# Four attention query tiles fewer, rotary halves exchanged on the keys, FFN operands normalised in place, and a finer start

## The chip, the cores and the metric

The kernel runs on one core of a Trainium2 chip. TensorE (PE) multiplies matrices into PSUM banks; VectorE (DVE), ScalarE (ACT) and GpSimd (POOL) work on tiles in SBUF; SyncE (SP) and POOL issue transfers. PEld is PE's loading of weights, which runs beside its matmuls. The metric is device time in microseconds (us) from start to end of one execution. Each engine runs its own instructions in the order in which the program's scheduler has written them, and waits for others through semaphores.

## The reference

One inference step of two layers on 384 tokens of 1024 features: 128 context tokens and 256 latent ones. Layer 0 has multi-head latent attention, layer 1 a Mamba-2 scan; each layer has a feed-forward network (FFN) of half weight before and after its mixer. Cut to what matters here:

```python
def ffn_half(x, shift, scale, gate, g, w_in, w_out):
    return x + 0.5 * gate * swiglu(adaln_input(x, g, shift, scale), w_in, w_out)
def adaln_input(x, g, shift, scale):
    return rmsnorm(x, g) * (1 + scale) + shift
def mla_project(h, w_in, q_norm, kv_norm, wq_b):
    q_a, kv_a, k_r = jnp.split(h @ w_in, [Q_LORA, Q_LORA + KV_LORA], axis=-1)
    q = (rmsnorm(q_a, q_norm) @ wq_b).reshape(b, l, MLA_HEADS, QK_HEAD)
# latent tokens: the last 32 of a head's 96 query columns, and the one rotary key, are turned
def apply_axial_rope(x, cos, sin):
    rot = jnp.stack([-xr[..., 1, :], xr[..., 0, :]], axis=-2)
    return (xr * cos + rot * sin).reshape(x.shape).astype(x.dtype)
# attention: softmax(q k / sqrt(96)) v, 16 heads; latent tokens see context and latent keys
```

All weights and data are float32. shift, scale and gate come from SiLU(cond) times a matrix of 18 sections of 1024 columns, for two conditions (context and latent).

## The kernel before

Features lie on the partitions, tokens in the columns. Stages follow each other: FFN 0.0, attention (`mla`), FFN 0.1, FFN 1.0, the scan layer (`ssm`), FFN 1.1. Every weight tile of 128 x 128 is streamed from memory in units of eight (`raw`, SP's queue), split into a rounded part and a rest (`whi` by ACT, `wlo` by DVE: `stream_split`, three units ahead), and the moving operand is split too (`xh` and `xl`), so that one product takes three matmuls, lines 124 to 126 in `wmm`: xh by wlo, xl by whi, xh by whi.

An FFN has 44 input tiles of 8 x 3 matmuls (`in_tile`) and 8 output tiles of 22 x 3 (`fo`). xh and xl hold x times (1 + scale) times g, made tile by tile when the residual of the stage before is added (`prep_x`), plus two columns with the shift, one for each kind of token: 386 columns. The RMS factor comes later (`norm_stat`: three small matmuls `rs`, a few column operations, and `spread`, a matmul `rb` that spreads them over the partitions, copied to `rext`); `evac` multiplies each result by `rext` and adds the shift's columns. `in_first_pair` runs the first two tiles so that `rs` can stand behind seven k steps. Between tiles DVE makes sums for later sections of the modulation (`mod_steps`, line 183; `Fill` spreads them). mla has the eight columns 56 to 64 of these.

At the start the first two sections are made on PE in four rounds (`mod_round`, 2 MB of `mod01` each), and three pairs of input tiles (`head`) run two k steps behind each round.

In mla, `q_a` makes the low-rank query operand without its RMS factor; a second `rstd` spreads it, and `rq` holds it times the rotary table. A query tile holds one head: 64 plain rows, 32 rotary ones, and the same 32 with halves exchanged, so one product with `rq` (`q_scale`) turns and normalises; the key tile `kext` repeats the turned key. The loop runs over eight pairs of heads: `kq` (key tile `k`, 6 matmuls; from pair 2 on two query tiles `q` of 12), then for each head transposes of the pair before (`ta`, `tb`), `scores` (`s0`, `s1`), softmax on DVE and ACT (`mx`, `p`, `sm`), and `pv`.

Of the kernel before, what the change touches and what calls it, by code (L numbers as in the profile page):

```python
# [15 lines left out]
P = 128  # L16
# [5 lines left out]
NX = 386  # L22
DFF = 2816
# [10 lines left out]
N_UNITS = 4 * FFN_UNITS + 27 + 57  # L34
MOD_SECS = 18

# [10 lines left out]
for _name, _n in (("ident", 128), ("ones", 128), ("triu", 128), ("tril", 128), ("sup", 128), ("slo", 128), ("sel", 4)):  # L47
    _TAB[_name] = (_off, _off + _n)
    _off += _n
# [4 lines left out]
def kernel(ctx, tc, xT_d, wstream, mod01, modw, crow_d, cst_d, tab_d, rope_d, ckvT_d, krT_d, h0_d,  # L54
# [13 lines left out]

    cst = pers.tile([P, N_CST], F32, tag="cst", name="cst")
    tab = pers.tile([P, N_TAB], F32, tag="tab", name="tab")  # L70
    xT = pers.tile([P, KT, NTOK], F32, tag="xT", name="xT")
    xh = pers.tile([P, KT, NX], F32R, tag="xh", name="xh")
    xl = pers.tile([P, KT, NX], F32R, tag="xl", name="xl")
    mod = pers.tile([P, 144, 2], F32, tag="mod", name="mod")
    gs = pers.tile([P, KT, 2], F32, tag="gs", name="gs")
    hg = pers.tile([P, KT, 2], F32, tag="hg", name="hg")
    cst32 = pers.tile([P, KT, 32], F32, tag="cst32", name="cst32")
    acc = pers.tile([P, NTOK], F32, tag="acc", name="acc")
    rext = pers.tile([P, NX], F32, tag="rext", name="rext")
    dg = pers.tile([P, NTOK], F32, tag="dg", name="dg")  # L80
# [10 lines left out]
    nc.vector.memset(cst32, 0.0)  # L91
# [39 lines left out]
    def mod_round(r, pool):  # L131
        raw = pool.tile([P, KT, 512], F32, tag="mod01", name=f"mod01_{r}", bufs=4)
        for i in range(4):
            nc.sync.dma_start(raw[:, 2 * i:2 * i + 2, :], mod01[r][:, 2 * i:2 * i + 2, :])

        def run():
            ks = slice(2 * r, 2 * r + 2)
            ps = bank(f"psmod_{r}")
            for kt in range(KT):
                g = kt % 4  # L140
                mm(ps[32 * g:32 * g + 32, :], cst32[:, kt, :], raw[:, kt, :], start=(kt < 4), stop=(kt >= 4),  # L141
                   tile_position=(0, 32 * g))
            sb = pool.tile([P, 512], F32, tag="modsb", name=f"modsb_{r}", bufs=2)
            nc.scalar.copy(sb, ps)
            yield
            pt = bank("modT")
            for q in range(4):
                nc.tensor.transpose(pt[:, q * P:(q + 1) * P], sb[:, q * P:(q + 1) * P], T("ident"))
            red = pool.tile([P, 4, 2], F32, tag="modred", name=f"modred_{r}", bufs=2)
            nc.vector.tensor_reduce(out=red, in_=pt.rearrange("p (b g z) -> p b z g", b=4, g=4)[:, :, 0:2, :],  # L150
                                    axis=AX.X, op=ALU.add)
            dst = mod[:, 0:2 * KT, :].rearrange("p (c k) s -> p c k s", c=2)
            mb = C("modb", 0, 2 * KT).rearrange("p (c k) -> p c k", c=2)
            for i in range(2):
                tt(out=dst[:, :, ks, i], in0=red[:, :, i].rearrange("p (c k) -> p c k", c=2), in1=mb[:, :, ks], op=ALU.add)
            prep_scale(0, 0, ks)
            prep_shift(0, 0, ks)
            for kt in (2 * r, 2 * r + 1):
                prep_x(kt)
            yield  # L160
        return run()
# [51 lines left out]
    def rstd(sq, inv_n, out):  # L213
# [3 lines left out]
        v, r, w = (pers.tile([P, 3], F32, tag=f"rs{i}", name=f"rs{i}", bufs=2) for i in range(3))  # L217
# [5 lines left out]
        stt(out=r, in0=w, scalar=1.5, op0=ALU.add, in1=r, op1=ALU.mult)  # L223
        for c in range(3):
            ts(out=dg[:, c * P:(c + 1) * P], in0=T("ident"), scalar1=r[:, c:c + 1], scalar2=None, op0=ALU.mult)
# [49 lines left out]
    def in_tile(keyf, m):  # L275
        ps = bank("in")
        for k in range(KT):
            wmm(ps[:, :NX], keyf(m, k), xh[:, k, :], xl[:, k, :], k == 0, k == KT - 1)
# [19 lines left out]
    def head_mm(keyf, tiles, k0):  # L298
        for m, ps in tiles:
            for k in (k0, k0 + 1):  # L300
# [836 lines left out]
```

## Time and profile before

| | |
|---|---|
| median of 3 runs | 1695.97 us (1695.53 to 1696.38) |
| the profiled execution | 1695.77 us, its span 1694.0 us |
| busy share of the span | PE 98%, DVE 74%, ACT 47%, POOL 12% |
| mean granted clock of PE | 0.991 |

A profile shows each instruction's engine, line, tiles and time. Matmuls overlap, so the sum of their durations says more than the time that passes; starts say how fast they follow each other. In a row of a view, `<-` behind the bracket names what ended an engine's idle time, and `x` the number of instructions that are taken together.

### The profile page before, as it was taken

The numbers are of one execution on the slowest core, as the hardware profiler recorded it, in microseconds if no ns is written. First come the engines' busy times: TensorE is split into PE (matmuls) and PEld (weight loads), VectorE is DVE, ScalarE is ACT, GpSimd is POOL, SyncE is SP. The second block draws the span as 40 slices with busy tenths as digits, with TensorE's granted clock in tenths as the row PEclk, the third lists the DMA queues.
The fourth block names the chain that finished last, engine by engine and source line by source line (L and its number), as shares of the span: only waits on it lengthen the run. The fifth ranks groups of instructions, "written<-read, shape, count | busy, mean of one in ns | idle before, by whom it ended". The sixth has DMA issues, their size and how long they took to land.

```text
span 1694.0 us, 25203 instructions
## 1 busy us (share of the span) xinstructions
PE 1655.4 (98%) x9616; PEld 1584.6 (94%) x9631; DVE 1254.1 (74%) x2069; ACT 791.7 (47%) x1308; POOL 196.1 (12%) x180
## 2 busy tenths in 40 slices
PE   7999999999999999999999999999998999999996
PEld 3899999987899999999999999988897999999996
DVE  3798889579868888986888897888876765444443
ACT  3533333455544333334333333787766644333332
POOL 0111100110001111000111100023222201111000
PEclk9999999999999999999999999999998999999998
DMA  9476667443245666664666574354433333333331
GB/s 349 172 228 210 206 203 235 131 151 101 75 164 183 204 206 202 214 229 157 208 205 205 193 241 164 121 166 134 141 122 119 97 125 123 125 125 125 124 125 50
DMA packets 88441, 281.99 MB, mean 166 GB/s; under 512 B 9836, under 2 KB 19900, under 8 KB 87808
## 3 DMA queue, kind: packets, MB, share of 16 engines
q1 hardware_dynamic: 86560, 274.26, 49.6%
q0 software_dynamic: 1104, 5.28, 0.9%
q8 instruction: 75, 1.23, 0.3%
q10 hardware_dynamic: 656, 0.85, 0.1%
q14 instruction: 46, 0.38, 0.1%
HBM read 276.06 MB, written 4.28 MB: 165 GB/s over the span
## 4 chain that ended last, share of the span: by engine, by line
PE 88%; DVE 5%; ACT 4%; DMA 2%; issue 1%; SPq 0%; POOL 0%; DVEq 0%; ACTq 0%
PE in L124 17%; PE in L126 17%; PE in L125 17%; PE fo L124 7%; PE fo L126 7%; PE fo L125 7%; DVE ca L662 2%; DMA cp<-ecum_d 2%; PE so L124 1%; PE so L125 1%; PE so L126 1%; ACT L769 1%; PE psmod L141 1%; PE wo L124 1%; PE pv L548 1%
## 5 line engine op out<-in xcount | busy, mean ns | idle before, releaser
L124 PE MATMUL in<-xh,wlo 128*128 128x386 f32 x1792 | 613.0, 343 | 3.6 <-ACT xh L246 3.1
L109 ACT CAST whi<-raw 128x1024 fp32r<-128x1024 f32 x348 | 365.3, 1050 | 526.2 <-issue 227.0
L126 PE MATMUL in<-xh,whi 128*128 128x386 f32 x1792 | 610.1, 341 | 0.0
L125 PE MATMUL in<-xl,whi 128*128 128x386 f32 x1792 | 608.3, 339 | 0.2 <-DVE xl L248 0.2
L110 DVE TENSOR_TENSOR wlo<-raw,whi 128x1024 fp32r<-128x1024 f32 x348 | 430.5, 1237 | 129.9 <-ACT whi L109 129.6
L124 PEld LDWEIGHTS in<-xh,wlo 128*128 128x128 f32 x1792 | 339.2, 189 | 10.6 <-issue 4.5
L125 PEld LDWEIGHTS in<-xl,whi 128*128 128x128 f32 x1792 | 339.8, 190 | 4.9 <-issue 2.4
L126 PEld LDWEIGHTS in<-xh,whi 128*128 128x128 f32 x1792 | 337.9, 189 | 3.7 <-issue 3.7
L125 PE MATMUL fo<-al,whi 128*128 128x384 f32 x704 | 236.7, 336 | 0.0
L124 PE MATMUL fo<-ah,wlo 128*128 128x384 f32 x704 | 236.7, 336 | 0.0
L126 PE MATMUL fo<-ah,whi 128*128 128x384 f32 x704 | 236.7, 336 | 0.0
L183 DVE CUSTOM_DVE_ANT_0 work<-modraw,crow,cst 128x1024 f32<-128x1024 f32 x144 | 185.3, 1288 | 20.6 <-POOL al L327 19.3
L327 POOL TENSOR_TENSOR al<-work,ah 128x384 fp32r<-128x384 f32 x88 | 111.2, 1263 | 749.6 <-ACT ah L326 736.2
L124 PEld LDWEIGHTS fo<-ah,wlo 128*128 128x128 f32 x704 | 132.0, 187 | 0.0
L125 PEld LDWEIGHTS fo<-al,whi 128*128 128x128 f32 x704 | 132.0, 187 | 0.0
L126 PEld LDWEIGHTS fo<-ah,whi 128*128 128x128 f32 x704 | 132.0, 187 | 0.0
L183 DVE CUSTOM_DVE_ANT_0 workout<-modraw,crow,cst 128x1024 f32<-128x1024 f32 x96 | 123.1, 1282 | 6.5 <-DMA modraw<-in_modw_dram 5.0
L326 ACT CAST ah<-work 128x384 fp32r<-128x384 f32 x88 | 45.3, 514 | 131.0 <-DVE work L324 131.0
L319 DVE TENSOR_TENSOR work<-in,rext 128x386 f32<-128x386 f32 x88 | 49.1, 558 | 69.7 <-PE in L126 67.8
L320 DVE TENSOR_TENSOR work<-in,rext 128x386 f32<-128x386 f32 x88 | 48.8, 554 | 45.3 <-PE in L126 45.3
L322 ACT ACTIVATE work<-work 128x128 f32<-128x128 f32 (+1 forms) x176 | 70.6, 447 | 4.5 <-DVE work L319 4.1
L324 DVE SCALAR_TENSOR_TENSOR work<-work 128x128 f32<-128x128 f32 (+1 forms) x176 | 68.0, 427 | 5.2
(257 smaller groups left out, 1683.4 us busy)
## 6 DMA issues: line engine op xcount, KB each, us to landing
raw<-in_w_dram SPq DMA_DIRECT2D x348, 512.0 KB, 3.8
modraw<-in_modw_dram SPq DMA_DIRECT2D x128, 512.0 KB, 4.4
mod<-in_mod_dram SPq DMA_DIRECT2D x16, 512.0 KB, 9.9
cp<-ecum_d SPq DMA_DIRECT2D x32, 256.0 KB, 5.0
crow<-silu_d POOLq DMA_DIRECT2D x4, 1024.0 KB, 6.1
h<-in_h_dram SPq DMA_DIRECT2D x16, 128.0 KB, 3.4
out_dram<-sto SPq DMA_DIRECT2D x16, 128.0 KB, 2.3
xT<-in_xT_dram SPq DMA_DIRECT2D x4, 384.0 KB, 9.3
```

The source lines that it names most:

```text
L109: nc.scalar.copy(his[u], raws[u])
L110: tt(out=los[u], in0=raws[u], in1=his[u], op=ALU.subtract)
L124: mm(out, wl, rh, start=start, stop=False)
L125: mm(out, wh, rl, start=False, stop=False)
L126: mm(out, wh, rh, start=False, stop=stop)
L183: nc.vector.tensor_tensor_reduce(out=junk(), in0=raw[n], in1=crow[:, s, :], scale=1.0, scalar=C("modb", j), op0=ALU.mult, op1=ALU.add, acc ...
L319: tt(out=g, in0=pg[:, :NX], in1=rext, op=ALU.mult)
L320: tt(out=u, in0=pu[:, :NX], in1=rext, op=ALU.mult)
L322: act(sg[:, a:b], g[:, a:b], AF.Silu, bias=g[:, NTOK + s:NTOK + s + 1])
L324: stt(out=sg[:, a:b], in0=u[:, a:b], scalar=u[:, NTOK + s:NTOK + s + 1], op0=ALU.add, in1=sg[:, a:b], op1=ALU.mult)
L326: nc.scalar.copy(ah[:, j, :], sg)
L327: nc.gpsimd.tensor_tensor(out=al[:, j, :], in0=sg, in1=ah[:, j, :], op=ALU.subtract)
```

## The change

- Start: `mod_round` becomes `FirstMod`, in rounds of one, one, two, two and two k tiles; the six head tiles run one k step at a time; a few matmuls on zeros (`busy`) and an early activation stand ahead.
- FFN: the first tiles (six in FFN 0.0, else four, `first_four`) run as before, k by k. While they run, `normed_x` overwrites xh and xl with the finished operand, RMS factor and shift included. All later input tiles have 384 columns, and their `evac` is one SiLU from PSUM, one product and the split. The first tiles keep the old one as `evac_raw`.
- Layout: rows of xh, xl and rext are 416 elements long, and small pads move the start of tiles.
- mla: twelve query tiles instead of sixteen: a tile `("n", p)` holds the plain rows of two heads, a tile `("r", g)` the rotary rows of four. `turn` multiplies the rotary tile by cos and by sin; `place` moves the rows of each head into its query operand, rows by DMA on POOL's queue and plain rows by ACT, for the pair behind the current one. The keys hold the halves exchanged. The query's RMS factor goes into the exponential as a scale for each token and into the maximum. The spread of it goes. The mod columns of mla go to FFN 0.0 (16 to 64 in place of 16 to 56).

```diff
+    def first_four(keyf, tiles, layer, sub):
+        ps = [bank(f"in{i}") for i in range(4)]
+        for k in range(KT):
+            for m, p in zip(tiles, ps):
+                wmm(p[:, :NX], keyf(m, k), xh[:, k, :], xl[:, k, :], k == 0, k == KT - 1)
+            if k == 1:
+                spread = norm_stat()
+            if k == 3:
+                spread()
+            if k >= 3:
+                for i in (range(4) if k == 3 else (k,)):
+                    normed_x(layer, sub, i)
+        return ps
+
+    def normed_x(layer, sub, k):
+        sh = sec(layer, 3 * sub)
+        t = pers.tile([P, NTOK], F32, tag="sq", name=f"xn{k}", bufs=2)
+        for s, a, b in SEGS:
+            stt(out=t[:, a:b], in0=xT[:, k, a:b], scalar=gs[:, k, s:s + 1], op0=ALU.mult, in1=rext[:, a:b], op1=ALU.mult)
+        for s, a, b in SEGS:
+            act(xh[:, k, a:b], t[:, a:b], AF.Identity, bias=sh[:, k, s:s + 1])
+        for s, a, b in SEGS:
+            stt(out=xl[:, k, a:b], in0=t[:, a:b], scalar=sh[:, k, s:s + 1], op0=ALU.add,
+                in1=xh[:, k, a:b], op1=ALU.subtract)
...
+            def evac(j, pg, pu):
+                sg = scratch(j)
+                act(sg, pg[:, :NTOK], AF.Silu)
+                tt(out=sg, in0=pu[:, :NTOK], in1=sg, op=ALU.mult)
+                product(j, sg)
...
+            def turn(g, pq):
+                turned[g] = mt([P, 2, NTOK], "qr", 1)
+                for x in range(2):
+                    tt(out=turned[g][:, x, :], in0=pq[:, :NTOK], in1=rope[:, x, :], op=ALU.mult)
+
+            def place(p, pq):
+                for i in range(2):
+                    h = 2 * p + i
+                    qs[h] = mt([P, NTOK], "qt", 4)
+                    a = 32 * (h % 4)
+                    for x in range(2):
+                        nc.gpsimd.dma_start(qs[h][64 + 32 * x:96 + 32 * x, :], turned[h // 4][a:a + 32, x, :])
+                    nc.scalar.copy(qs[h][0:64, :], pq[64 * i:64 * i + 64, :NTOK])
...
-                if qs is None:
-                    qs = []
-                    for h in (0, 1):
-                        pqh = bank("q")
-                        q_mm(pqh, 2 * p + h, range(4))
-                        qs.append(q_scale(pqh))
-                return qs
+                if 1 <= p < HEADS // 2 - 1:
+                    if p % 2 and p > 1:
+                        turn((p + 1) // 2, q_tile(("r", (p + 1) // 2)))
+                    place(p + 1, q_tile(("n", p + 1)))
...
-                    act(pt[:, a:b], s, AF.Exp, bias=mx[:, i:i + 1], scale=ATT_SCALE, accum_out=sm[:, i:i + 1])
+                    act(pt[:, a:b], s, AF.Exp, bias=mx[:, i:i + 1], scale=prq[:, i:i + 1], accum_out=sm[:, i:i + 1])
...
-            fill = Fill(mod_steps(mods[0], mods[1], lp, lambda: work[0][:, 896:]), HEADS // 2 - 1, 1)
```

Three places show how the instructions stand. First DVE at the entry of FFN 0.1, before, from the RMS factors (`dg`) to the first results (`work` from the first pair of tiles):

```order
L225 TENSOR_SCALAR dg<-tab,rs_4588 128x128 x3
L110 TENSOR_TENSOR wlo_4603<-raw_4420,whi_4602 128x1024
L110 TENSOR_TENSOR wlo_4633<-raw_4460,whi_4632 128x1024
L110 TENSOR_TENSOR wlo_4664<-raw_4500,whi_4663 128x1024
L319 TENSOR_TENSOR work_4703<-in_4560,rext 128x386
```

And the same place in the changed kernel, its beginning (`xn` is the scratch of `normed_x`, L305 its first and L309 its last pair of instructions):

```order
L237 TENSOR_SCALAR dg<-tab,rs_4581 128x128 x3
L109 TENSOR_TENSOR wlo_4618<-raw_4441,whi_4617 128x1024
L305 SCALAR_TENSOR_TENSOR xn_4626<-xT,gs,rext 128x128
L305 SCALAR_TENSOR_TENSOR xn_4626<-xT,gs,rext 128x256
L305 SCALAR_TENSOR_TENSOR xn_4633<-xT,gs,rext 128x128
L309 SCALAR_TENSOR_TENSOR xl<-xn_4626,mod,xh 128x128
L305 SCALAR_TENSOR_TENSOR xn_4633<-xT,gs,rext 128x256
L309 SCALAR_TENSOR_TENSOR xl<-xn_4626,mod,xh 128x256
```

Between the factors and the first results there were weight splits alone; now there are 32 instructions of `normed_x` more, of which six stand here; the product of the first result stands among them, ahead of the last xl.

Second, PE in the changed kernel at the same entry, in the two tiles behind the first four (`in_4762` is input tile 2, `in_4799` tile 24, which used to stand whole behind it):

```order
L123 MATMUL in_4762<-xh_62,wlo95_4618 128x384
L123 MATMUL in_4799<-xh_62,wlo96_4686 128x384
L124 MATMUL in_4799<-xl_63,whi96_4685 128x384
L125 MATMUL in_4799<-xh_62,whi96_4685 128x384
L123 MATMUL in_4799<-xh_62,wlo96_4686 128x384
L124 MATMUL in_4799<-xl_63,whi96_4685 128x384
L125 MATMUL in_4799<-xh_62,whi96_4685 128x384
L124 MATMUL in_4762<-xl_63,whi95_4617 128x384
L125 MATMUL in_4762<-xh_62,whi95_4617 128x384
```

The first row is k = 4 of tile 2 by xh; six matmuls of tile 24 stand between it and the two that need xl of k = 4. The two tiles stay interleaved so up to k = 7.

Third, POOL's queue in mla. Before, behind the copies of the turned key:

```order
L468 COPY kext_2794<-krot 64x384
L462 DMA out_dram<-kva 128x2x128
L179 DMA crow<-silu_d 128x2048 x2
```

and in the changed kernel:

```order
L535 COPY kext_2828<-krot 64x384
L502 DMA qt<-qr 32x384 x2
L529 DMA out_dram<-kva 128x2x128
L502 DMA qt<-qr 32x384 x30
L186 DMA crow<-silu_d 128x2048
```

The 32 transfers that move turned rows (`qr`) into the query operands (`qt`) stand there in a row, ahead of the load that the next FFN's mod sums need.

## Rows read from the trace of the kernel before

**Rows 1.** The page: span, and busy us (share) of three engines.

```profile
span 1694.0 us, 25203 instructions
PE 1655.4 (98%) x9616; PEld 1584.6 (94%) x9631; DVE 1254.1 (74%) x2069; ACT 791.7 (47%) x1308; POOL 196.1 (12%) x180
```

**Rows 2.** Windows, FFN 0.1 and 1.0, PE alone: busy (instructions), clock, DMA share, GB/s.

```profile
690.00:770.00 80.00, 80.00 (x460) 1.00 0.65 222
800.00:960.00 160.00, 160.00 (x906) 1.00 0.62 202
```

**Rows 3.** Window of one loop pair: busy (instructions) of PE, PEld, DVE, ACT, POOL.

```profile
422.70:434.70 12.00, 12.00 (x73) 9.71 (x72) 11.14 (x30) 6.44 (x18) 0.00 (x0) 1.00 0.25 88
```

**Rows 4.** Timeline of PE, one loop pair: first query matmul, first transpose behind.

```profile
398.74 0.34 PE L124 MATMUL q<-qph,wlo 128*128 128x384 f32 x1
...
402.93 0.49 PE L534 MATMUL ta<-tab,p 128*128 128x128 f32 x3
```

**Rows 5.** Line 183, mod sums in the loop: ns min/median/max, first and last start.

```profile
L183 DVE CUSTOM_DVE_ANT_0 p<-modraw,crow,cst x16: 1272/1277/1285, 382.7 to 448.9; 128x1024 f32<-128x1024 f32 x16
```

**Rows 6.** Timeline of PE, pair 1: last key matmul and the transposes behind.

```profile
376.36 0.40 PE L126 MATMUL k<-ckvh,whi 128*128 128x512 f32 x1
378.33 0.33 PE L534 MATMUL ta<-tab,p 128*128 128x128 f32 x1 [1.57 <-DVE p L526]
```

**Rows 7.** Timeline of PE where the query factors are spread.

```profile
358.07 0.88 PE L229 MATMUL rb<-dg,tab 128*128 128x384 f32 x2
358.50 0.69 PE L484 MATMUL v<-wlo,ckvh 128*128 128x512 f32 x1
```

**Rows 8.** DMA issues on POOL's queue: count, KB each, median us to landing.

```profile
kext<-in_krT_dram POOLq DMA_DIRECT2D x4, 32.0 KB, 2.6
```

**Rows 9.** Timeline of PE at the start.

```profile
5.55 1.92 PE L141 MATMUL psmod<-mod,cst 128*32 128x512 f32 x4 [5.55 <-DMA mod<-in_mod_dram]
8.10 4.45 PE L141 MATMUL psmod<-mod,cst 128*32 128x512 f32 x12 [0.63 <-DMA mod<-in_mod_dram]
...
16.96 0.66 PE L124 MATMUL in<-xh,wlo 128*128 128x386 f32 x1 [3.08 <-ACT xh L246]
...
21.29 0.69 PE L124 MATMUL in<-xh,wlo 128*128 128x386 f32 x1
...
22.71 1.05 PE L141 MATMUL psmod<-mod,cst 128*32 128x512 f32 x4
23.69 0.44 PE L126 MATMUL in<-xh,whi 128*128 128x386 f32 x1
```

**Rows 10.** Window in the start, columns as rows 3.

```profile
15.00:20.00 5.00, 3.04 (x8) 1.94 (x10) 4.21 (x7) 3.73 (x8) 0.00 (x0) 0.52 1.03 410
```

**Rows 11.** Timeline at the entry of FFN 1.0, whose first matmul starts at 775.21.

```profile
776.41 0.80 ACT L246 ACTIVATE xh<-xT,gs 128x128 fp32r<-128x128 f32 x2
777.68 0.74 DVE L248 SCALAR_TENSOR_TENSOR xl<-xT,gs,xh 128x128 fp32r<-128x128 f32 x2
779.04 0.80 PE L216 MATMUL rs<-tab,acc 128*128 128x1 f32 x6
779.70 0.42 PE L124 MATMUL in<-xh,wlo 128*128 128x386 f32 x1
780.56 1.06 ACT L109 CAST whi<-raw 128x1024 fp32r<-128x1024 f32 x1 [0.29 <-PE in L126]
781.70 1.22 DVE L110 TENSOR_TENSOR wlo<-raw,whi 128x1024 fp32r<-128x1024 f32 x1
```

**Rows 12.** Line 319, a product with `rext`: columns as rows 5.

```profile
L319 DVE TENSOR_TENSOR work<-in,rext x88: 547/560/564, 64.5 to 1582.1; 128x386 f32<-128x386 f32 x88
```

**Rows 13.** Windows behind the wait of pair 1, and in the scan layer.

```profile
378.00:382.00 4.00, 3.46 (x21) 2.55 (x22) 3.51 (x11) 2.84 (x10) 0.00 (x0) 1.00 0.01 4
...
1274.00:1278.00 4.00, 1.88 (x11) 1.55 (x12) 3.22 (x5) 3.25 (x7) 0.00 (x0) 0.59 0.11 33
1278.00:1282.00 4.00, 4.00 (x16) 3.96 (x15) 1.73 (x5) 0.07 (x1) 1.25 (x1) 0.55 0.59 190
```

More of the change, by code (lines that the diff above doesn't have):

```diff
@@ L157, in run @@
             prep_shift(0, 0, ks)
[L158 to L161, printed above, removed]
+            for k in range(k0, k0 + n):
+                prep_x(k)
     silu_d = tc.dram_tile([2, 1024], F32, name="silu_d")
@@ L223, in rstd @@
         stt(out=r, in0=w, scalar=1.5, op0=ALU.add, in1=r, op1=ALU.mult)
+        return r
+    def rstd(sq, inv_n, out):
+        r = rstd_cols(sq, inv_n)
+        dg = pers.tile([P, NTOK], F32, tag="sq", name="dg", bufs=2)
         for c in range(3):
@@ L460, in mla @@
                 tt(out=ckvl[:, i, 0:NTOK], in0=kva[:, i, :], in1=ckvh[:, i, 0:NTOK], op=ALU.subtract)
-            spread = rstd(qacc, 1.0 / 512.0, qacc)
+            rcol = rstd_cols(qacc, 1.0 / 512.0)
+            for i, c in enumerate((1, 2, 0)):
+                ts(out=prq[:, i:i + 1], in0=rcol[:, c:c + 1], scalar1=ATT_SCALE, scalar2=None, op0=ALU.mult)
+            ts(out=nrq[:, 0:3], in0=prq[:, 0:3], scalar1=-1.0, scalar2=None, op0=ALU.mult)
+            turn(0, p_r0)
+            place(0, p_n0)
             nc.gpsimd.dma_start(cache_d[0:256, :].rearrange("(a p) t -> p a t", p=P), kva[:, :, 0:NCTX])
@@ L468, in mla @@
                 nc.gpsimd.tensor_copy(kext[i][64:128, 0:NTOK], krot[64:128, :])
-            for h in (2, 3):
-                pq.append(bank("q"))
-                q_mm(pq[h], h, range(4))
-            spread()
-            tt(out=rq, in0=qacc, in1=rq, op=ALU.mult)
+            p_n1 = q_tile(("n", 1))
+            p_r1 = q_tile(("r", 1))
+            place(1, p_n1)
             for half in range(2):
@@ L492, in mla, with kq @@
                 if half == 0:
-                    qs0 = [q_scale(pq[h]) for h in range(4)]
-            def kq(p, qs):
+                    turn(1, p_r1)
+            def kq(p):
                 ps = bank("k")
@@ L566, in mla @@
                         pTs.append(transposes(prev[h]))
[L567 removed]
+                    new.append(scores(2 * p + h, qs.pop(2 * p + h)))
                 if prev is not None:
@@ L1025, in _weights @@
         elif kind == "q":
-            _, h, k = key
-            cols = [h * 96 + i for i in range(96)] + [h * 96 + 64 + i for i in swap]
+            _, (what, t), k = key
+            if what == "n":
+                cols = [h * 96 + i for h in (2 * t, 2 * t + 1) for i in range(64)]
+            else:
+                cols = [h * 96 + 64 + i for h in range(4 * t, 4 * t + 4) for i in range(32)]
             src = wq[rows(k)][:, cols]
```

277 lines of the change are left out of this document (157 added, 120 removed).

## The prediction

> **What bounds the kernel now.** I read the page's busy times first: TensorE (PE) is busy for 98% of the span, VectorE (DVE) for 74% [rows 1]. Busy PE alone says little, so I next looked for PE waits, matmul by matmul. Inside the four feed-forward (FFN) stages it is at work without a break, 160.00 of 160 us and 80.00 of 80 [rows 2]; it waits at the start, in pairs 0 and 1 of the attention loop, in some steps of the scan layer, and at the end. So the price of a matmul is its pitch, from start to start, not the duration of 336 or 343 ns that the page prints for one (they overlap). Stretches inside one stage give it: 906 matmuls of 386 columns in 160 us, 460 of 384 columns in 80 us [rows 2]. Two matmuls of each count hang over an edge, so the pitch is 160/904 = 177.0 ns and 80/458 = 174.7 ns. The attention loop looks different, with DVE busy for 11.1 of 12 us, but PE is busy for all 12 [rows 3]: PE is the limit there too, with DVE close behind. What counts is therefore how many PE instructions go, and which new waits come.
>
> **The change part by part.**
>
> *Query tiles.* 48 matmuls of 384 columns go: the loop makes 8 tiles of 12 instead of 12 tiles (the four tiles ahead of the loop stay four). The 24 of one pair now take 398.74 to 402.93, 4.19 us, 174.6 ns each [rows 4]. **-8.4**. It counts in full if PE stays the limit. DVE loses work too: the sixteen mod sums of 1.28 us in the loop [rows 5], and one of two query products a pair. They move to the FFN stages, 16 sums of 1.28 us each beside some 320 us of PE work, where each tile pair also loses one product and two short ones on DVE; I cost them at nothing, cover PE's matmuls; without cover they are 20 us.
>
> *Waits in the loop.* In pair 1 PE starts its last k matmul at 376.36 and the next instruction at 378.33, 1.97 us later; 1.57 of it is idle, ended by the weights p of the first softmax [rows 6]. The changed order puts a query tile of 12 matmuls, 2.1 us, there; between the idle 1.57 and the whole 1.97 I take -1.7. The last pair loses all its query work, and its scores may wait for the copies of k: +0.5, my estimate; bounds 0 and 2 (the wait of pair 1). **-1.2**.
>
> *Query norm.* The spread of its factors over the partitions goes: 358.07 to 358.50 on PE [rows 7], **-0.4**. The small columns that replace it lie under the value tiles.
>
> *Rotary halves.* 32 DMAs on POOL's queue bring the turned rows into the query tiles. Transfers of like size on that queue land 2.6 us after issue [rows 8], and they go out one pair, some 10 us, ahead of use; the cover is that pair. Cost 0. Behind them on POOL stands nothing that the loop needs, but the single buffer for turned rows makes DVE wait for them once, ahead of the second half of the value tiles.
>
> *384 columns for 386 in the FFN stages.* With operands normalised in place, 40 of 44 input tiles (38 in the first stage) need no bias columns: (38 + 3 x 40) x 24 = 3,792 matmuls. I price each at the difference of the two pitches, 2.3 ns [rows 2]: **-8.7**. Rows of 384 columns, 1,536 bytes, start at multiples of 64 bytes, as the changed ones of 1,664 bytes will; those of 386, 1,544 bytes, mostly don't. The part that is columns alone is bounded below by 2/386 of 177.0 ns, 0.9 ns, which gives -3.5. On this the Trainium skill (TensorE: Matmul & The Clock Gate, section Back-to-back issue gap) has a rule that would make the gain smaller: a matmul alone takes its columns at 2.4 GHz plus 2.5 ns. By it 386 and 384 columns differ by 0.8 ns, and this term would be -3.2; the measured pitches are some 12 ns above the rule for either, so I go by the rows. The 1,584 matmuls that keep 386 columns get aligned rows: 0 to -3.6 (2.3 ns each); many are in the scan layer, where other engines limit; **-1**.
>
> *Start.* PE runs densely from 21.29 on. Before that it did 20 records of mod sums, four transposes and six matmuls [rows 9], which at the later rate (four records in 0.98, from 22.71 to 23.69) and with three transposes in 0.49 [rows 4] are 4.9 + 0.7 + 1.1 = 6.7 us; 14.6 were lost, part of it at a granted clock of 0.52, almost wholly the lower of its two levels, 1.2 GHz [rows 10]. The first round now loads half: its sums took 5.55 to 12.55, half of 7.0 is 3.5, so they end near 9.1, and with the chain of 4.4 us from the sums' end to the first matmul (12.55 to 16.96) the first matmul comes at about 13.5. By then 2.4 us of work are done: 11.1 lost, and half a microsecond more, my estimate, for a clock that falls again in this gap: **-3.0**, bounds 0 and -8 (all of the chain but its first half gone).
>
> *Entries of the FFN stages.* This is what the change adds. Normalising one of the eight operand tiles takes DVE two pairs of instructions, each as long as the pair that makes xl, 0.74 us, with a pair of 0.80 on ACT between [rows 11]: 1.48 a tile, 11.8 for eight. In a later stage the first four tiles take 12 matmuls for each k. The 48 of k = 0 to 3 and the sums end at 48 x 0.176 + 0.66 = 9.1 us after entry. Then a weight split stands ahead on both engines, 1.06 on ACT and 1.22 on DVE: normalising begins at 11.4. With two more splits, one product of 0.56 [rows 12] and 0.3 for hand-overs it ends at 11.4 + 11.8 + 2.4 + 0.6 + 0.3 = 26.5. PE is through the four tiles at 9.1 + 0.4 + 8.4 = 17.9 and would be through the next two at 26.3. The order interleaves these two, so that ten matmuls, 1.75 us, are left when the last operand is there: 28.3. That is a wait of 2.0 us, three times. In the first stage six tiles share each k and the factors come at k = 6. There 31 + 48 matmuls, 13.9 us, lie between factors and the end of the two tiles; DVE needs 1.0 + 11.8 + 2.4 + 0.3 = 15.5, and seven matmuls, 1.2, follow: 2.8. **+8.8**, bounds 0 and 24 (four times 6: if the second tile did not fill in, the last operand, due at 17.9 + 22 x 0.175 = 21.7, would be 4.8 late, and a little clock with it).
>
> Sum: -8.4 - 1.2 - 0.4 - 8.7 - 1.0 - 3.0 + 8.8 = **-13.9**. The profiled execution took 1695.77 us, beside a span of 1694.0 [rows 1] and a median of 1695.97; I forecast **1682**.
>
> **Rivals.**
>
> *Slower: the entries cost more than all the rest saves.* The rest is 22.7, so from 5.7 us an entry nothing is gained, and 0.2% is lost from 6.5. The place is DVE's queue at entry; the mechanism is the 4.8 above (no fill-in) and PE falling to half clock after it. For it: in the scan layer, where PE worked for only 1.88 of 4 us, the granted clock went to 0.59 and stayed at 0.55 while PE was busy again for 4.00 of 4.00 [rows 13]; half of 4 us is 2 lost, with half of the slow part before it 3. Against: after the 1.97 us of pair 1 the clock was 1.00 [rows 13], and the waits here come in pieces of 1.6 us and less. 4 x (4.8 + 3.0) = 31: 1704.
>
> *Free entries.* DVE keeps up, since hand-overs overlap better than I count: 1682 - 8.8 + 1 = 1674. For it: pitch and waits in the old stages show no stall at all. Against: 15 us of DVE work against 15 us of PE.
>
> *The pitch doesn't follow the rows.* Columns alone: 5.2 to 5.5 less is gained, and the aligned rest gains nothing: 1688.
>
> *The rotary halves come late.* The Trainium skill (SBUF — State Buffer, section SBUF: two separate sides) says that a DMA issued from GpSimd waits while DVE holds the port pair that they share, in a 2-port instruction. No run here shows it for these DMAs. As a mechanism of this kernel: eight DMAs go out ahead of the value tiles' second half, and DVE's product for the next group waits for them in the single buffer. If each took the landing time of 2.6 us in turn [rows 8], 21 us against about 8 of value and key work, PE would lose some 13 us: 1695, within 0.2% of no change. Such transfers have stood ahead of nothing in a hurry so far, so the rows are silent.
>
> **How the numbers follow.** A measurement of this kernel tells 0.2%, 3.4 us, from no change. Forecast with 1 to 4 us at each entry 0.52; free entries 0.17; pitch smaller 0.14; late halves 0.07; entries that decide 0.10 (half of it not past 0.2%). Faster 0.84, same 0.08, slower 0.08. The likeliest case alone reaches from 1676 to 1688. Free entries together with a start 4 us better give the low end, 1670; small pitch together with one more microsecond at each entry gives the high end, 1692.
>
> **What would show it.** Right: 384-column input matmuls at a pitch of 174 to 175 ns; pairs 2, 4 and 6 of the loop some 2 us shorter than 12.0 and pairs 3 and 5 as long as before; no wait after the k tile of pair 1; at each FFN entry PE waits of 1 to 4 us in all, released by DVE's xl, in the two tiles behind the first ones. Wrong: loop pairs that stay at 12 us; PE waiting for qt or for vt; a granted clock under 1.00 in the first 30 us of an FFN stage after the first; a first matmul after 15 us.

## The result, and the profile after

The changed kernel takes 1678.43 us (median of 4 runs, 1675.54 to 1680.10) against 1696.12 us before: a ratio of 0.9894 (95% interval 0.9877 to 0.9911), 17.7 us less. The forecast was 1682, with 1670 to 1692 as its range. The profiled execution is the shortest of the four, with a span of 1673.8 us against 1694.0 [rows 1]: 20.2 us to be placed. Several terms of the forecast were off by some us, on both sides.

The page, the same lines as in [rows 1]:

```profile
span 1673.8 us, 25075 instructions
PE 1626.8 (97%) x9592; PEld 1558.0 (93%) x9607; DVE 1227.8 (73%) x1952; ACT 793.3 (47%) x1309; POOL 228.0 (14%) x211
```

PE's share fell by one per cent: some waits are new. Windows of PE in the output tiles of FFN 0.1 and the input tiles of FFN 1.0 (columns as in [rows 2]), first of the changed kernel:

```profile
680.00:740.00 60.00, 60.00 (x348) 1.00 0.72 233
800.00:940.00 140.00, 140.00 (x810) 1.00 0.68 218
```

Counted as in the prediction, the input tiles go at 140/808 = 173.3 ns and the output tiles at 60/346 = 173.4. Counted over all starts (waits left out) it is 176.95 before and 173.33 now for input tiles, and 174.67 and 173.33 for output tiles. So the input tiles gained 3.6 ns a matmul, not 2.3, and the output tiles, at which nothing was edited but where their operands lie, gained 1.3 ns.

One loop pair that makes only a tile of plain rows, and one that makes both kinds, as windows (columns as in [rows 3]):

```profile
388.00:398.00 10.00, 10.00 (x61) 7.68 (x61) 7.58 (x23) 8.11 (x24) 0.00 (x0) 1.00 0.06 13
398.00:410.00 12.00, 12.00 (x73) 9.71 (x72) 8.65 (x21) 8.78 (x20) 3.94 (x8) 1.00 0.41 116
```

The first has 12 PE instructions fewer than [rows 3] and is 2 us shorter, the second has as many and is as long. DVE, busy for 11.14 of 12 us before, now has room in both. In the same stage, the wait of pair 1 [rows 6]: PE's timeline there.

```profile
380.41 0.33 PE L125 MATMUL q<-qph,whi 128*128 128x384 f32 x1
380.62 0.33 PE L596 MATMUL ta<-tab,p 128*128 128x128 f32 x1
```

Between the last query matmul and the transposes there is 0.21 us. The tile that was put there covers the softmax.

The time that was lost stands in FFN 0.0. A window from behind its entry to the end of its input tiles, of the changed kernel (columns as in [rows 3]):

```profile
77.00:227.00 150.00, 142.96 (x811) 139.77 (x810) 141.69 (x185) 50.70 (x71) 26.50 (x19) 1.00 0.74 235
```

and the like stretch before:

```profile
77.00:224.00 147.00, 147.00 (x833) 147.00 (x832) 130.91 (x202) 57.33 (x88) 22.94 (x18) 1.00 0.65 208
```

Before, PE had no break there. Now it is idle for 7 us and more is lost around each wait: at 173.3 ns, 150 us would hold 865 matmuls, and 809 start in it (two of the 811 hang over an edge), so 9.7 us are missing. DVE is busy for 141.69 of 150 us. Who waits for whom, by the view of waits (us in total, times, longest) in this window:

```profile
PE in L123 <- DVE wlo L109: 7.0, 9, 1.3
```

PE waits for weight splits, though DVE's work in this stage should have been hidden. The timeline at one of these places shows why they are late (most rows of PE, PEld and ACT are left out):

```profile
126.51 1.27 DVE L190 CUSTOM_DVE_ANT_0 work<-modraw,crow,cst 128x1024 f32<-128x1024 f32 x1
126.62 0.51 ACT L354 CAST ah<-work 128x384 fp32r<-128x384 f32 x1 [6.37 <-DVE work L377]
127.21 1.45 POOL L355 TENSOR_TENSOR al<-work,ah 128x384 fp32r<-128x384 f32 x1 [7.78 <-ACT ah L354]
127.71 2.03 DVE L109 TENSOR_TENSOR wlo<-raw,whi 128x1024 fp32r<-128x1024 f32 x1
129.79 0.44 PE L123 MATMUL in<-xh,wlo 128*128 128x384 f32 x1 [0.98 <-DVE wlo L109]
```

POOL's subtraction for `al` runs from 127.21 to 128.66. The split that starts at 127.71 beside it takes 2.03 us, where 1.22 is usual: its end, 129.74, is 1.08 behind POOL's end, so it did next to nothing until POOL was through. Grouped by line, DVE in this window (busy, mean ns, idle before):

```profile
L190 DVE CUSTOM_DVE_ANT_0 work<-modraw,crow,cst 128x1024 f32<-128x1024 f32 x63 | 84.2, 1343 | 5.3 <-DMA modraw<-in_modw_dram 4.7
L109 DVE TENSOR_TENSOR wlo<-raw,whi 128x1024 fp32r<-128x1024 f32 x35 | 52.4, 1498 | 1.2 <-ACT whi L108 1.2
```

A split takes 1,498 ns in the mean. The 18 that met no instruction of POOL took 1.22. Of the 17 that met one, the 12 that started while it ran took 2.02 to 2.08 us, and the 5 that were already running when it started took 1.22 as ever. Of the 63 sums, the 5 that started while it ran took 2.03 to 2.05 in place of 1.28. Together that is some 13.5 us of DVE's time. Such a meeting shows as a long duration, not as a wait.

The kernel before has the same subtraction (line 327), and in its window it cost DVE only some 2 us. What mostly started beside it there was the product of line 319, which has one of its inputs in PSUM. From its timeline:

```profile
118.73 1.44 POOL L327 TENSOR_TENSOR al<-work,ah 128x384 fp32r<-128x384 f32 x1 [6.51 <-ACT ah L326]
...
119.23 0.56 DVE L319 TENSOR_TENSOR work<-in,rext 128x386 f32<-128x386 f32 x1
```

Eleven of these products started while POOL's instruction ran, and each took 0.55 or 0.56 us, as all of them do [rows 12]. The change takes them out of the later tiles; in the changed kernel what starts beside POOL in this window is splits and sums, which have both inputs in SBUF, and the short reads of a sum's result.

The Trainium skill (SBUF — State Buffer, section SBUF: two separate sides) describes this: DVE and GpSimd share a port pair, and an instruction of DVE with two inputs in SBUF and one of GpSimd that reads SBUF shut each other out for the whole instruction. The trace agrees (2.03 us for a split that starts beside POOL, 1.22 without). The prediction had weighed this very section against transfers and not against line 355, where it counts.

At the start, windows of PE from 15 to 20 and 25 to 30 us:

```profile
15.00:20.00 5.00, 5.00 (x33) 0.75 0.98 417
25.00:30.00 5.00, 2.35 (x20) 1.00 1.03 433
```

From 15 to 20 us PE is at work throughout (3.04 of 5 us before, at a clock of 0.52, [rows 10]), but from 25 to 30 us for less than half the time. The first input matmul starts at 13.51 (16.96 before, [rows 9]). The 145th input matmul, the first behind the six head tiles, starts at 56.55 (62.43 before).

### The profile page after: what moved, and what is told of

Same layout as the page of the kernel before. It is cut to its first block, busy times and chain, and to the rows that moved or that the text cites. A ratio compares the mean times of both kernels' runs of the same rounds, so it can differ in the third digit from the quotient of the medians.

```text
span 1673.8 us, 25075 instructions
## 1 busy us (share of the span) xinstructions
PE 1626.8 (97%) x9592; PEld 1558.0 (93%) x9607; DVE 1227.8 (73%) x1952; ACT 793.3 (47%) x1309; POOL 228.0 (14%) x211
## 4 chain that ended last, share of the span: by engine, by line
PE 80%; DVE 9%; ACT 4%; DMA 3%; issue 3%; POOL 0%; SPq 0%; DVEq 0%; ACTq 0%
PE in L123 14%; PE in L124 14%; PE in L125 14%; PE fo L123 7%; PE fo L125 7%; PE fo L124 7%; DVE ca L720 2%; DMA modraw<-in_modw_dram 2%; DVE wlo L109 2%; DVE work L190 2%; PE so L123 1%; PE so L125 1%; PE so L124 1%; DMA cp<-ecum_d 1%; ACT L827 1%
## 5 line engine op out<-in xcount | busy, mean ns | idle before, releaser
L123 PE MATMUL in<-xh,wlo 128*128 128x384 f32 (+1 forms) x1792 | 606.3, 341 | 14.5 <-DVE wlo L109 10.8
L124 PE MATMUL in<-xl,whi 128*128 128x384 f32 (+1 forms) x1792 | 604.8, 338 | 1.0 <-DVE xl L309 0.6
L125 PE MATMUL in<-xh,whi 128*128 128x384 f32 (+1 forms) x1792 | 603.0, 337 | 0.0
L109 DVE TENSOR_TENSOR wlo<-raw,whi 128x1024 fp32r<-128x1024 f32 x346 | 454.4, 1313 | 189.4 <-ACT whi L108 189.2
L123 PEld LDWEIGHTS in<-xh,wlo 128*128 128x128 f32 x1792 | 336.9, 189 | 25.1 <-DVE wlo L109 11.6
L355 POOL TENSOR_TENSOR al<-work,ah 128x384 fp32r<-128x384 f32 x88 | 127.4, 1447 | 719.1 <-ACT ah L354 719.1
L190 DVE CUSTOM_DVE_ANT_0 work<-modraw,crow,cst 128x1024 f32<-128x1024 f32 x160 | 210.4, 1318 | 18.7 <-POOL al L355 13.1
L377 DVE TENSOR_TENSOR work<-in,work 128x384 f32<-128x384 f32 x79 | 43.8, 555 | 57.8 <-PE in L125 57.8
L720 DVE SCALAR_TENSOR_TENSOR ca<-u,cst,ca 128x386 f32<-128x386 f32 x96 | 71.0, 749 | 2.2 <-ACT ca L718 1.6
L258 ACT ACTIVATE xh<-xT,gs 128x128 fp32r<-128x128 f32 x96 | 41.2, 452 | 64.3 <-DVE xT L320 64.3
L320 DVE SCALAR_TENSOR_TENSOR xT<-fo,hg,xT 128x128 f32<-128x128 f32 x64 | 24.4, 412 | 31.6 <-PE fo L125 31.6
```

The lines of the kernel that those rows point to most:

```text
L109: tt(out=los[u], in0=raws[u], in1=his[u], op=ALU.subtract)
L123: mm(out, wl, rh, start=start, stop=False)
L124: mm(out, wh, rl, start=False, stop=False)
L125: mm(out, wh, rh, start=False, stop=stop)
L190: nc.vector.tensor_tensor_reduce(out=junk(), in0=raw[n], in1=crow[:, s, :], scale=1.0, scalar=C("modb", j), op0=ALU.mult, op1=ALU.add, acc ...
L258: act(xh[:, kt, a:b], xT[:, kt, a:b], AF.Copy, scale=gs[:, kt, s:s + 1])
```

## The experiments

Each kernel was timed against the kernel before, whose medians beside them were 1695.48 to 1696.10 us. Where a comparison with the changed kernel is given, it is the difference of medians to its 1678.4; that one was timed only once (4 runs), so a difference of a microsecond or two to it says nothing. The start differs by up to 3 us between profiles of kernels with the same start (56.55 to 59.77 for the 145th matmul in ten of them), so differences of single stages are read from the profiles.

**The sums back in the loop.** FFN 0.0 makes mod columns 16 to 56 again, and the attention loop 56 to 64, as before the change, with a scratch tile of their own.

```diff
+            junk = lp.tile([P, 1024], F32, tag="junk", name="junk")
+            fill = Fill(mod_steps(mods[0], mods[1], lp, lambda: junk), HEADS // 2 - 1, 1)
...
+                fill()
+            fill(True)
...
-    ffn(0, 0, (16, 48, 64), (0, 1), head)
-    mla((0, 2))
+    ffn(0, 0, (16, 40, 56), (0, 1), head)
+    mla((56, 64), (0, 2))
```

> The changed kernel with the mod columns 56 to 64 (16 sums on DVE) taken back from FFN 0.0 into the attention loop. Theory A: in FFN 0.0 those sums make DVE late with the weight splits, and PE waits some 12 us for them in the profile of the changed kernel; without them these waits fall under 2 us, and the loop has room (DVE 60.6 of 86 us busy, 20.5 more): 1668 to 1671. Rival B: a loop pair of 10 us has no room for 2.3 sums more on DVE and grows by 1 us or more each: the gain is given back, 1676 to 1680. Rival C: the waits in FFN 0.0 come from the normalising at its entry and stay: 1678 or more.

Measured: 1675.75 us (1673.21 to 1677.60), ratio 0.9878 (0.9864 to 0.9891). Window of the same stretch of FFN 0.0, and the one long wait in the loop, on PE's timeline:

```profile
77.00:227.00 150.00, 148.56 (x854) 147.60 (x853) 128.88 (x165) 55.04 (x77) 28.30 (x20) 1.00 0.67 215
```

```profile
374.01 0.33 PE L125 MATMUL q<-qph,whi 128*128 128x384 f32 x1
379.72 0.48 PE L596 MATMUL ta<-tab,p 128*128 128x128 f32 x1 [5.38 <-DVE p L588]
```

FFN 0.0 gets 43 of its 56 missing matmuls back: from its 145th input matmul to its first output tile it is 162.48 us in place of 171.09, 8.6 less. Theory A holds there, and rival C falls. But the attention stage gives back 7.2 us (175.31 in place of 168.07), not in all pairs as rival B had it: in one place. With a scratch tile of their own the sums depend on nothing in the loop, the scheduler puts six of them on DVE between 364.9 and 379.3 us, ahead of the end of the first softmax, and PE stands until 379.72.

**The attention part alone.** The kernel before with all of the change in `mla`, sums in the loop in the place that they had.

```diff
-N_UNITS = 4 * FFN_UNITS + 27 + 57
+N_UNITS = 4 * FFN_UNITS + 25 + 57
...
+            def turn(g, pq):
...
+            def place(p, pq):
...
                 pt = work[0] = lt([P, 896 + 1024], "p")
```

> The kernel before with the attention part of the change alone (12 query tiles, rotary halves by transfers, query factor in the exponential); the 16 sums stay in the loop, the FFN stages and the start are as before. Theory A: the attention stage saves the 10.0 us that it saves in the changed kernel, from PE work alone: 1685 to 1687. Rival B: part of that gain came from taking the sums out of the loop, since DVE has 11.1 of 12 us before; with them in it the short pairs stay near 11 us: 1689 to 1692.

Measured: 1686.61 us (1685.67 to 1687.64), ratio 0.9943 (0.9930 to 0.9955). The first input matmul of the attention stage and that of FFN 0.1, before:

```profile
316.34 0.34 PE L124 MATMUL in<-xh,wlo 128*128 128x386 f32 x1
...
494.65 0.34 PE L124 MATMUL in<-xh,wlo 128*128 128x386 f32 x1
```

in the changed kernel:

```profile
319.15 0.34 PE L123 MATMUL in<-xh,wlo 128*128 128x386 f32 x1
...
487.22 0.34 PE L123 MATMUL in<-xh,wlo 128*128 128x386 f32 x1
```

and in the attention part alone:

```profile
317.79 0.34 PE L123 MATMUL in<-xh,wlo 128*128 128x386 f32 x1
...
485.94 0.34 PE L123 MATMUL in<-xh,wlo 128*128 128x386 f32 x1
```

178.31, 168.07 and 168.15 us. The gain is PE work and needs no sums taken out: theory A. It also says that the move of the sums into FFN 0.0 bought the attention stage nothing.

**386 columns again.** Input tiles behind the first ones compute 386 columns; the last two are not used.

```diff
-                pg = in_tile(keyf, j, NTOK)
+                pg = in_tile(keyf, j)
```

(and the same for `pu`).

> The changed kernel, but the later input tiles compute 386 columns again (the last two are not used); rows stay 1,664 bytes apart. Theory A: the pitch fell from 177.0 to 173.3 ns mostly because rows are aligned; two columns alone are 0.9 ns: pitch 174.2, 3,792 matmuls, 3.4 us more: 1681 to 1683. Rival B: the number of columns sets the pitch, by more than its share: pitch 176 to 177, 10 to 14 us more: 1688 to 1692.

Measured: 1696.03 us (1693.63 to 1697.99), ratio 0.9997 (0.9988 to 1.0005): 17.6 more than the changed kernel. Windows of PE in output and input tiles:

```profile
700.00:760.00 60.00, 60.00 (x341) 1.00 0.68 219
800.00:940.00 140.00, 140.00 (x794) 1.00 0.64 207
```

Input tiles go at 140/792 = 176.8 ns (176.67 over all starts): rival B, 3.3 ns for two columns, 3,792 x 3.3 = 12.7 us. What nobody had expected is the first row: the output tiles, whose 384 columns and places in memory are those of the changed kernel, go at 176.67 instead of 173.33 ns. That is 1.76 us a stage, 7.0 in all. The two together are 19.7 us, more than either theory had and near the 20.2 between the two profiles.

**Rows of 386 elements.** The other half of the layout: columns as in the change, rows as before.

```diff
-XROW = 416
+XROW = 386
```

> The changed kernel with rows of 386 elements (1,544 bytes) in place of 416 in the moving operands of the input tiles; 384 columns as in the change. Theory A: unaligned rows cost most of what was gained: pitch near 176 ns, 8 to 11 us more: 1686 to 1690. Rival B: rows don't matter, the columns did it: within 2 us of the changed kernel, 1677 to 1680.

Measured: 1688.63 us (1687.10 to 1691.94), ratio 0.9958 (0.9944 to 0.9971).

```profile
690.00:750.00 60.00, 60.00 (x346) 1.00 0.70 229
800.00:940.00 140.00, 140.00 (x800) 1.00 0.65 211
```

Input tiles 175.4 ns by the window (175.56 over all starts), output tiles 174.67: 3,792 x 2.2 = 8.5 and 2.8 us, close to the 10.2 measured and inside theory A. The shorter rows also move what lies behind them in memory, the operands of the output tiles and the weights among them, so this is not the rows alone. With the run ahead it says that either half of the edit alone would have brought at most 1.4 of the 3.6 ns.

**Last pair at 386 columns.** To see whether the output tiles take their pitch from what ran ahead of them.

```diff
+                n = NX if j == NFF - 1 else NTOK
-                pg = in_tile(keyf, j, NTOK)
+                pg = in_tile(keyf, j, n)
```

(and the same for `pu`).

> The changed kernel, in which only the last pair of input tiles of each FFN stage computes 386 columns (48 matmuls of 1,056); the output tiles are untouched, at the same places in memory. Theory A: the output tiles take over the pitch of what ran ahead of them: 176.7 ns in place of 173.3 as behind stages of 386 columns, 2,112 matmuls, 7 us more: 1684 to 1687. Rival B: the pitch of the output tiles is a matter of their own operands, and what differed with all tiles at 386 columns was something else: 173.3 ns, 0.6 us for the 192 matmuls: 1678 to 1680.

Measured: 1689.12 us (1686.25 to 1690.15), ratio 0.9956 (0.9942 to 0.9969).

```profile
690.00:750.00 60.00, 60.00 (x342) 1.00 0.69 227
```

60/340 = 176.5 ns by the window, 176.67 over all starts, in all four stages. Theory A: 48 matmuls of 386 columns ahead make the next 528 matmuls slower by 3.3 ns each, at the same operands. It explains 7.0 of the 10.7 us; the profile's start was 2.9 us later than that of the changed kernel.

This is not a rule for every tile behind 386 columns, as the changed kernel itself shows. In each later FFN stage its first four tiles, 96 matmuls, have 386 columns, and the input tiles behind them have 384. At the passage in FFN 0.1 (PE, the first, the 6th and the 12th matmul of 384 columns):

```profile
505.49 0.34 PE L123 MATMUL in<-xh,wlo 128*128 128x384 f32 x1
...
506.37 0.33 PE L125 MATMUL in<-xh,whi 128*128 128x384 f32 x1
...
507.41 0.34 PE L125 MATMUL in<-xh,whi 128*128 128x384 f32 x1
```

The first five steps take 0.88 us, 176 ns each; the next six take 1.04, 173.3 each, without a wait between. It is the same in the other two stages. So in the input tiles the slower pitch was gone after six matmuls, and in the output tiles it stayed for 528. No run here tells what makes the difference.

**No pad.** The operands of the output tiles start 64 bytes earlier.

```diff
-            fp.tile([P, 16], F32, tag="pad", name="pad")
```

> The changed kernel without the pad of 64 bytes ahead of the FFN operands ah and al, so that their rows start at multiples of 128 bytes as in the kernel before. Theory A: where the operands start sets the pitch of the output tiles: it goes from 173.3 back to 174.7 ns, 2,112 matmuls, 2.8 us: 1680 to 1683. Rival B: the pitch of the output tiles is taken over from the input tiles ahead of them (176.7 behind tiles of 386 columns at the same places in memory): it stays at 173.3: 1677 to 1680.

Measured: 1686.15 us (1682.93 to 1689.11), ratio 0.9941 (0.9926 to 0.9955).

```profile
690.00:750.00 60.00, 60.00 (x343) 1.00 0.70 225
```

The output tiles go at 176.00 ns: neither the 174.7 of theory A nor the 173.3 of rival B. The direction is A's, 1.42 us a stage, 5.7 of the 7.7 us measured. So both count, where the operands lie and what ran before.

**Less in the input tiles of FFN 0.0.** Four mod columns (8 sums) go from its input tiles to its output tiles.

```diff
-    ffn(0, 0, (16, 48, 64), (0, 1), head)
+    ffn(0, 0, (16, 44, 64), (0, 1), head)
```

> The changed kernel; in FFN 0.0 four sections (8 sums) are moved from the input tiles to the output tiles. Theory A: DVE is over its capacity in the input tiles (the waits for weight splits cost 8.6 us against the kernel with 16 sums fewer there) and has 14 us to spare in the output tiles (77.0 of 91 busy): the waits shrink by 4 to 6 us, the output tiles stay as they are: 1672 to 1675. Rival B: the output tiles, too, are bound by the order of DVE's work, or by the loads of the mod rows, and give it back: 1677 to 1681.

Measured: 1674.88 us (1674.33 to 1676.70), ratio 0.9879 (0.9866 to 0.9891). The waits of PE in the input tiles, and in the output tiles:

```profile
PE in L123 <- DVE wlo L109: 3.6, 4, 1.3
```

```profile
PE fo L123 <- DVE wlo L109: 1.1, 2, 0.6
```

The input tiles win 5.9 us, the output tiles lose 2.4: theory A in the first, some of rival B in the second.

**The low part on DVE in FFN 0.0.** If POOL's instruction stops DVE for its whole length, DVE loses nothing by doing that work itself.

```diff
-                nc.gpsimd.tensor_tensor(out=al[:, j, :], in0=sg, in1=ah[:, j, :], op=ALU.subtract)
+                eng = nc.vector if head is not None else nc.gpsimd
+                eng.tensor_tensor(out=al[:, j, :], in0=sg, in1=ah[:, j, :], op=ALU.subtract)
```

> The changed kernel; in FFN 0.0 the low part of each product (line 355) is made on DVE in place of POOL: 22 instructions of some 0.5 us more on DVE, 11 us. Theory A: DVE cannot work while POOL's instruction runs (17 sums and 17 splits that met it took 1.50 and 1.79 us in place of 1.28 and 1.22, 13.5 us in all), so DVE loses nothing by doing it itself and wins 2 us: 1675 to 1679. Rival B: the long durations beside POOL are only apparent, since DVE would have waited for something else anyway; then DVE, already late, is later by 8 to 11 us, and so is PE: 1685 to 1690.

Measured: 1670.66 us (1668.43 to 1672.03), ratio 0.9851 (0.9838 to 0.9863), 7.8 less than the changed kernel. The window, DVE by line (line 355 is line 356 here), and the waits of PE:

```profile
77.00:227.00 150.00, 149.50 (x863) 149.18 (x862) 144.47 (x217) 53.19 (x74) 0.00 (x0) 1.00 0.76 249
```

```profile
L190 DVE CUSTOM_DVE_ANT_0 work<-modraw,crow,cst 128x1024 f32<-128x1024 f32 x63 | 80.2, 1280 | 4.2 <-DMA modraw<-in_modw_dram 3.8
L109 DVE TENSOR_TENSOR wlo<-raw,whi 128x1024 fp32r<-128x1024 f32 x37 | 45.1, 1219 | 0.6 <-ACT whi L108 0.6
L356 DVE TENSOR_TENSOR al<-work,ah 128x384 fp32r<-128x384 f32 x20 | 11.0, 552 | 0.0
```

```profile
PE in L123 <- DVE wlo L109: 0.8, 2, 0.5
```

Every split takes 1.22 us again and every sum 1.28. DVE does 11.0 us of work more, is busy for only 2.8 more, and PE has 863 matmuls in the window instead of 811. From the 145th input matmul to the first output tile it is 161.56 us in place of 171.09. The gain is larger than theory A said, which had counted DVE's time alone and not the matmuls that no longer wait for it.

**The low part on DVE in all four stages.** Line 355 as above, but without the condition.

```diff
-                nc.gpsimd.tensor_tensor(out=al[:, j, :], in0=sg, in1=ah[:, j, :], op=ALU.subtract)
+                tt(out=al[:, j, :], in0=sg, in1=ah[:, j, :], op=ALU.subtract)
```

> The changed kernel with the low part of each product made on DVE in all four FFN stages (in FFN 0.0 alone it gave 1670.7). Theory A: in the three later stages DVE has room, the longer splits beside POOL are hidden behind PE's work, so nothing more is gained: 1669 to 1672. Rival B: the longer splits cost PE something there too, in waits under the 0.35 us that were looked at: 1665 to 1668. Rival C: DVE's work at the entries grows by some 0.5 us for each early product, and the entries, free by a hair, begin to cost: 1672 to 1676.

Measured: 1669.25 us (1667.36 to 1671.49), ratio 0.9842 (0.9828 to 0.9855), the fastest here. The three later stages keep their lengths (185.0 to 185.1 us of input tiles): theory A, the longer splits were hidden there; the 1.4 us to the last kernel are within what two kernels of one start differ by.

**The first pair of each normalised tile twice.**

```diff
-        for s, a, b in SEGS:
+        for s, a, b in SEGS * 2:
             stt(out=t[:, a:b], in0=xT[:, k, a:b], scalar=gs[:, k, s:s + 1], op0=ALU.mult, in1=rext[:, a:b], op1=ALU.mult)
```

> The changed kernel, but the first pair of DVE instructions of each normalised tile runs twice: 0.66 us a tile, 5.3 us an entry, four entries. Theory A: the entries are free by a hair (the last operand was there 25.0 us after entry, and PE wanted it some 24.6 after): PE waits 4 to 5.3 us more at each: 1694 to 1700. Rival B: there is slack, since other tiles can be brought forward: 1679 to 1687.

Measured: 1697.38 us (1695.94 to 1703.72), ratio 1.0015 (1.0007 to 1.0024), 19.0 more than the changed kernel. The input tiles of the four stages grow by 2.6, 6.6, 6.6 and 3.7 us. In FFN 0.1:

```profile
523.56 0.34 PE L125 MATMUL in<-xh,whi 128*128 128x384 f32 x1
526.69 0.69 PE L123 MATMUL in<-xh,wlo 128*128 128x384 f32 x1 [2.79 <-DVE wlo L109]
```

Theory A: there is next to no slack, and what is late in the end is a weight split behind the operands in DVE's queue.

**Rounds of two at the start.** Four equal rounds, k tiles one by one as in the change; the order of the loads, and the places of the rounds' sums between the k tiles, go with it.

```diff
-ROUNDS = ((0, 1), (1, 1), (2, 2), (4, 2), (6, 2))
+ROUNDS = ((0, 2), (2, 2), (4, 2), (6, 2))
```

> The changed kernel with four rounds of two k tiles each at the start, in place of five of one, one, two, two and two; k tiles are still taken one by one and nothing else differs. Theory A: the small first rounds bring the first input matmul forward by some 3 us, and that is most of what the start gained: the 145th input matmul comes 3 us later than the 56.5 to 59.8 of the profiles so far, and the time is 1680 to 1683. Rival B: the start is bound by the bytes that have to arrive (some 430 GB/s until 35 us), whatever the rounds: within 1 us, 1677 to 1680.

Measured: 1682.76 us (1680.45 to 1682.97), ratio 0.9918 (0.9904 to 0.9931), 4.3 more. The 145th input matmul comes at 61.45 us, later than in all ten profiles with the small rounds. Theory A: the small rounds are most of what the start gained.

**No matmuls on zeros.**

```diff
-        busy(4)
...
-        busy(1)
```

> The changed kernel without the five matmuls on zeros at the start. Theory A: they do nothing for the time; the granted clock falls in the gap ahead of the first input matmul with or without them: 1677 to 1680. Rival B: they keep the clock up through 10 to 25 us; without them this stretch is at the lower level as in the kernel before (0.52 from 15 to 20 us): 2 to 4 us more, 1680 to 1683.

Measured: 1677.05 us (1676.29 to 1678.82), ratio 0.9889 (0.9875 to 0.9902); 145th input matmul at 58.01 us. From 15 to 20 us the granted clock is 0.82 without them (0.75 with them, 0.52 in the kernel before). Theory A: they do nothing for the time that could be told here.

## Why the prediction was right, point by point

| term | forecast | measured, us |
|---|---|---|
| query tiles, loop waits, query norm | -10.0 | -10.2 (178.31 to 168.07); -10.2 alone |
| 384 columns | -8.7 | -13.7 (3,792 x 3.62 ns) |
| aligned rows of the rest | -1.0 | -1.3 (the scan layer, 342.01 to 340.71; its input tiles' pitch 176.9 to 176.7 explains 0.3) |
| start | -3.0 | -5.9 (145th input matmul) |
| entries of the FFN stages | +8.8 | some +3 in the first stage, 0.2 in each of the other three |
| 16 sums moved to FFN 0.0, beside POOL's part | 0 | some +9.5 (171.09 to 161.56 without POOL's part; to 162.48 without the sums) |
| output tiles | not in the sum | -2.8 (4 x 0.71) |
| end | not in the sum | +0.5 |

The measured column adds to -20.3, beside 20.2 between the spans. The 0.2 is what is left in the later stages: their input tiles are 3.3 us shorter, where 960 x 3.62 ns would be 3.5.

*Attention.* Right in mechanism and size. Pairs 2, 4 and 6 take 9.9 us and pairs 3 and 5 12.0, as said; the wait of pair 1 is gone. The 32 transfers of rotary rows landed 2.7 us after issue in the median, 4.5 at most (forecast 2.6), and no wait of PE in this stage names a query operand, so the late rotary halves did not come.

*384 columns.* Right in direction, too small in size, and the price rested on an idea that failed. The term took the pitch of the output tiles, 174.7 ns, for that of 384 columns. The experiments show that there is no such thing as the pitch of 384 columns: 173.33, 174.67, 175.56, 176.00 and 176.67 ns were all measured with them. Nor do aligned rows alone do it: 386 columns went from 176.95 to 176.67 with them, and the prediction had allowed up to 2.3 ns. By the rule of the Trainium skill that the prediction weighed (TensorE: Matmul & The Clock Gate, section Back-to-back issue gap) the gain would have been 3.2 us; the trace does not agree, at 13.7. The pitches of the rows were 13.7 and 12.2 ns above that rule, not some 12 for either as the prediction has it.

*Entries.* The mechanism is there, the size was not. Normalising in FFN 0.1, on DVE's timeline:

```profile
498.83 1.00 DVE L305 SCALAR_TENSOR_TENSOR xn<-xT,gs,rext 128x128 f32<-128x128 f32 x3
499.75 0.34 DVE L309 SCALAR_TENSOR_TENSOR xl<-xn,mod,xh 128x128 fp32r<-128x128 f32 x1
...
511.06 1.14 DVE L309 SCALAR_TENSOR_TENSOR xl<-xn,mod,xh 128x256 fp32r<-128x256 f32 x3
```

It begins 11.6 us after the first matmul of 487.22 (forecast 11.4) and ends at 512.20, 25.0 after it (forecast 26.5). The step that failed is the sum of durations: instructions on DVE overlap, 1.00 us of three is followed by the next 0.92 later. The prediction had warned of this for PE and then did it for DVE. 1.5 us was most of the 2.0 us of waiting that it had worked out: behind the two tiles that follow the first four, PE went on 26.95 us after the first matmul (forecast 28.3), 0.4 later than without any waits. In FFN 0.0 the 301st input matmul starts 30.2 us behind the 145th, where 156 pitches are 27.0: some 3 us, near the 2.8 of the forecast. The doubled normalising shows that the entry was on the edge: 5.3 us more on DVE cost up to 6.6.

*The sums.* This step failed outright: 16 sums at nothing, with PE's matmuls as cover. A cover is time in which DVE is free, and DVE had little in that stage: 130.91 of 147 us were busy before the change. The prediction did not read this window. It set some 320 us of PE's work beside the sums, but all sixteen came into the input tiles of FFN 0.0, some 160 us. The bound without cover, 20 us, was stated but kept out of the range. And it counted the products that go as a gain for DVE alone; with them went what had stood beside POOL's subtraction without loss, and DVE's loss to POOL grew from 2 to 13.5 us. Sums and subtraction together made DVE late: without the sums 8.6 us came back, and without the subtraction on POOL 9.5, though DVE got more work.

*Start.* The small rounds act as said; the forecast was low. Over the ten profiles with this start the 145th matmul comes at 58.1 us in the mean, against 62.4 and 63.9 in the two of the old start, so about 5 us are the size, not 5.9. Of these some 3.4 lie ahead of the first input matmul (14.2 in the mean against 17.0 and 18.1), near the 3.0 of the forecast, and the rest behind it. The runs of the changed kernel spread over 4.6 us and those of the kernel before over 0.9 beside them, but over 5.3 in 15 runs at another time, so the spread is no mark of the change. Where it comes from was not settled.

*Signs.* Two of the signs that the prediction named did not come: the pitch was 173.3 ns and not 174 to 175, and behind the first stage no entry shows PE waits of 1 to 4 us. What came in three of four stages is its rival of free entries, at 0.17, and not its likeliest case.

So that the forecast of 1682 came near is partly luck: the 9.5 us lost that it did not see stand against 5.2 too much at the entries and 5.0, 2.9 and 2.8 too little gained at the columns, the start and the output tiles.

## What to carry to other kernels

Work that is moved to an engine off the critical path needs that engine's busy time in the very stage that gets it, and the instructions of other engines that shut it out; here the cure was to take work from POOL and give it to the busier engine. Before an instruction is taken out, see what will then stand beside the other engines in its place. Price instructions from start to start on every engine, not only on the one that limits. After an edit to one kind of matmul, read the pitch of the kinds behind it as well.

## What the runs showed of the hardware

The pitch of a matmul of 384 columns is not settled by its shape. The output tiles, with one layout, ran at 173.33 ns through a whole stage behind tiles of 384 columns and at 176.67 behind as few as 48 matmuls of 386, four times out of four each. Where operands start counts too: 176.00 without the pad ahead of the low and high parts, 173.33 with them 64 bytes further. Which combination gives which pitch could not be told from these runs. In the output tiles a pitch stayed until the stage ended; in the input tiles of the changed kernel that of 386 columns was gone after six matmuls of 384.

A split or a sum of DVE, both with two inputs in SBUF, that starts while POOL's subtraction runs makes next to no way until it is through: 2.03 us for a split that takes 1.22 alone. One that is already running when POOL starts keeps its 1.22, and a product with one input in PSUM keeps its 0.56. In FFN 0.1 and 1.0 of the changed kernel this costs DVE some 9 us each and PE nothing: without it the input tiles of both stages were as long as with it.
